# First weight sums of the down projections: added by GpSimd's DMAs from DRAM to DRAM instead of by VectorE, and three more seven-product pairs

## The chip, the cores and the metric

The kernel runs on one core of one Trainium2 chip. The metric is the device time of one execution in microseconds; of the kernel before there are three runs: 2095.61, 2094.24 and 2094.99 us, median 2094.99.

## What is computed

A two-layer encoder trunk on one sequence of 256 tokens, width 2048, all in float32. Per layer: an RMS norm, one input projection, a token mixer (layer 0 differential attention, layer 1 windowed grouped-query attention with a sink) beside four heads that attend to 256 memory tokens, an output projection, and an MLP with squared ReLU. Cut to what the change touches:

```python
for i in range(DEPTH):                      # 2 layers
    h = rms_norm(x, norm_attn[i])
    proj = h @ w_in_a[0]                    # layer 0: 2048 x 5120; layer 1: w_in_b, 2048 x 3072
    ...                                     # heads, memory heads (w_mem_kv)
    x = x + heads @ w_out[i]                # 2048 x 2048
    h = rms_norm(x, norm_mlp[i])
    x = x + jnp.square(jax.nn.relu(h @ w_up[i])) @ w_down[i]   # 2048 x 8192, then 8192 x 2048
```

## The kernel before, in words

**Products in three passes.** Every float32 operand is split into a rounded part and a rest (`split`, L411 to L413: ScalarE copies `hi`, VectorE subtracts to get `lo`), and each product is three TensorE matmuls (`three`, L503: hi by hi, hi by lo, lo by hi). Weights come from DRAM in pieces of 512 KB (128 partitions x 1024 float32), by DMAs that SyncE issues (`fetch`, L389) into four buffers `raw`; four `hi` and four `lo` buffers follow. The order of the pieces is one long plan (L254 to L259): per layer the input projection (`a`, 80 pieces, or `b`, 48), the memory projection (16 pieces), `out`, `up` (128 pieces), `down` (128 pieces). A piece of an input projection feeds 12 matmuls of 512 columns (`chunk_tok`, L453 to L469).

**Down projection.** Each half of the output columns (h = 0, 1) goes through 32 pairs of pieces (j = 0 to 31). A pair is a 2 x 2 block product for two column chunks and two token tiles: normally eight block products, 24 matmuls (`one_of_eight`, L508). For the pairs in `FAST` (L48; `LATE`, L49, for the second half of layer 0) it is done with seven products, 21 matmuls (`seven`, L521), in the manner of Strassen and Winograd. These need two sums of weights, a and b, and differences of the hidden values. There are 15 + 13 + 15 + 15 = 58 such pairs.

**Weight sums.** For a seven-product pair `load_pair` (L316) has SyncE load the first piece whole into a slot of the tile `big`. `sum_pair` (L336) makes a (first piece, its two halves, each plus the upper half of the second piece: `first_sum`, L281, one VectorE addition over 1024 columns), then b by two additions over 512 columns, and splits both. For 19 of the 58 pairs (`MADE`, `MADE_LATE`: 5 + 4 + 5 + 5) a is not made there: `make_sum` (L284) loads the three halves a second time during the up projection, adds on VectorE (L302, the same L282), and GpSimd's DMAs store the sum to DRAM (`madesum`, L307, two of 256 KB). `load_pair` then loads that sum (512 KB) and only the lower half of the second piece (256 KB, tile `t2k`), instead of the whole second piece. A pair whose sum is in DRAM so takes 1.25 MB of loads, any other 1 MB.

**Hidden differences.** `keep` (L962) makes the differences of the hidden values for every pair j that is a seven-product pair in either half, during the up projection, and a GpSimd DMA stores them (`kept`, L967, 512 KB); in the down projection a GpSimd DMA loads them (L1038). Six buffers `h2` carry both, and the split hidden values.

**Order.** PE, VectorE, ScalarE, GpSimd and SyncE each have one queue. The program text interleaves side work with the pieces through a small planner: `tick` is called once per piece in the input projections, and a `Task` does its next stage when its wait, counted in ticks, is over; `Light` stages are done beside the others. That sets the place in the text. The build then lays each engine's instructions out by when their inputs and buffers are there; where a load or an operation must not come earlier than its place, the text says so with `tc.issue_after` (L292, L377, L745, L755, L824, L1079, L852), which queues it behind a named instruction of the same engine.

**Bias.** Around the place of the change in layer 0, GpSimd also makes position distances (`bias_distance`, L751) and issues 32 DMAs of 128 KB (`bias_hot`, L796) for the relative-position bias. TensorE multiplies what they bring (`bias_rows`, L806).

Of the kernel before, what the change touches and what calls it, by code (L numbers as in the profile page):

```python
# [14 lines left out]
F32 = mybir.dt.float32  # L15
# [4 lines left out]
ALU = mybir.AluOpType  # L20
# [24 lines left out]
SINGLE = 4  # L45
AHEAD = 2
WARM = 10
FAST = (1, 3, 5, 7, 9, 11, 13, 15, 17, 19, 21, 23, 25, 27, 29)  # L48
LATE = (3, 5, 7, 9, 11, 13, 15, 17, 19, 21, 23, 25, 27)  # L49
AWAY = range(6, 12)  # L50
LATE_BLK = (9, 13, 17, 21, 25)
LOOK = 2
KEEP_AFTER = (2, 6)
MADE_GAP = 1
MADE = (3, 9, 15, 21, 27)
MADE_LATE = (7, 13, 19, 25)
LAM_INIT = 0.8 - 0.6 * math.exp(-0.3 * 0)

G_ATTN, G_MEM, G_MLP = 0, 2 * KT, 4 * KT
# [9 lines left out]
def trunk(ctx: ExitStack, tc: tile.TileContext, xin, xtok, memin, memtok, posrel, gcol, rows,  # L69
# [43 lines left out]
    def t2k(shape, dt=F32):  # L113
        return tp.tile(shape, dt, tag="t2k", name=nm("t2k"), bufs=6)
# [127 lines left out]
            return LATE if (name, h) == ("down0", 1) else FAST  # L242
        return ()

    def made_pairs(name, h):

        if name.startswith("down"):
            return MADE_LATE if (name, h) == ("down0", 1) else MADE
        return ()

    def plan_pairs(name, n):
        plan.extend((name, h, j) for h in range(2) for j in range(2 * n))

# [27 lines left out]
    def first_sum(a, first, upper):  # L281
        nc.vector.tensor_tensor(a, first.rearrange("p (a n) -> p a n", a=2), upper.unsqueeze(1).broadcast_to([P, 2, 512]), op=ALU.add)  # L282

    def make_sum(name, h, j):  # L284

        box = {}

        def load(i):
            if i == 0:
                box["raw"] = quad("h2", (P, 1024), F32), t2k([P, 512])  # L290
            first, upper = box["raw"]
            with tc.issue_after(behind[0].ins):  # L292
                if i < 2:
                    nc.sync.dma_start(first[:, i * 512:(i + 1) * 512], weights[name][h, 2 * j][:, i * 512:(i + 1) * 512])
                else:
                    nc.sync.dma_start(upper, weights[name][h, 2 * j + 1][:, 512:1024])

        def add():
            first, upper = box["raw"]
            box["a"] = quad("h2", (P, 2, 512), F32)  # L300
            box["kept"] = dp.tile([P, 2, 512], F32, name=nm("madesum"))
            first_sum(box["a"], first, upper)  # L302
            made_in[name, h, j] = box["kept"]
            save(0)

        def save(i):
            nc.gpsimd.dma_start(box["kept"][:, i, :], box["a"][:, i, :])  # L307

        return Task([lambda: load(0), lambda: load(1), lambda: load(2), add, lambda: save(1)], gap=MADE_GAP)

    made_in = {}
    hidden_in, hids = {}, {}
# [639 lines left out]
    def mlp(layer, X2, last):  # L952
        hT = []
        kept = {}
        wide = big([P, 6, 4, S])
        slots.clear()
        slots.extend(wide[:, c - 6] for c in AWAY)
        hidden_in.clear()
        def hidden(j):
            return hT[j // 2].rearrange("p k s -> p (k s)")[:, (j % 2) * 512:(j % 2) * 512 + 512]  # L960

        def keep(j):  # L962

            t2 = quad("h2", (P, 2, 512))
            differences(t2, hidden(j))
            kept[j] = dp.tile([P, 2, 512], F32R, name=nm("kept"))
            nc.gpsimd.dma_start(kept[j], t2)  # L967

        to_make = [(f"down{layer}", h, j) for h in range(2) for j in made_pairs(f"down{layer}", h)]
        for c in range(16):  # L970
            for i in range(len(to_make) * c // 13, len(to_make) * (c + 1) // 13):
                if i < len(to_make):
                    make_sum(*to_make[i])
            ps = chunk_out(f"up{layer}", c, 8, lambda k: X2[k], "mm" if c % 2 == 0 else "aux", 2 if c == 0 else 1)
            if c == 0:
                mlp_stats()
            ht = wide[:, c - 6] if 6 <= c < 12 else blk([P, 4, S], F32)
            for o in range(4):
                t = t1k()
                nc.scalar.copy(t, ps[o][:, 256:512])  # L980
                nc.vector.tensor_tensor(t, ps[o][:, 0:256], t, op=ALU.add)
                nc.vector.scalar_tensor_tensor(ht[:, o, :], t, 0.0, t, op0=ALU.max, op1=ALU.mult)
            hT.append(ht)
            if c in AWAY:
                for i in range(2):
                    hidden_in[2 * c + i] = dp.tile([P, 512], F32, name=nm("hid"))
                    nc.gpsimd.dma_start(hidden_in[2 * c + i], hidden(2 * c + i))
            for j in (2 * c, 2 * c + 1):
                if any(j in fast_pairs(f"down{layer}", h) for h in range(2)):
                    Task([Light(lambda j=j: keep(j), 0)], wait=KEEP_AFTER[j % 2])  # L990
        N2 = Halves()

        def h2_of(j):
            t2 = quad("h2", (P, 2, 512))
            split(t2[:, 0, :], t2[:, 1, :], hids.pop(j) if j in hidden_in else hidden(j))
            return lambda kk, t, part: t2[:, part, kk * S + t * P:kk * S + (t + 1) * P]

        flush()

        for half_ in range(2):  # L1000
            tag = "mm" if half_ == 0 else "aux"
            ps = [[bank(tag) for _ in range(2)] for _ in range(2)]
            chunks = (2 * half_, 2 * half_ + 1)
            fast = fast_pairs(f"down{layer}", half_)

            def add_to(n, t, src, i=0):
                at = chunks[n] * 512 + i
                d = xt[:, t, at:at + src.shape[1]]
                nc.vector.scalar_tensor_tensor(d, src, r2[:, t:t + 1], d, op0=ALU.mult, op1=ALU.add)
                return at, d  # L1010

            def finish(n, t, src, i=0):
                at, d = add_to(n, t, src, i)
                if last:
                    nc.sync.dma_start(out[:, t * D + at:t * D + at + src.shape[1]], d)

            def by_columns(n, t):

                for i in (0, 256):
                    part_ = bank("mm")[:, 0:256]  # L1020
                    for j, two, at in held:
                        for kk in range(2):
                            three(part_, j == held[0][0] and kk == 0, j == held[-1][0] and kk == 1,
                                  lambda part: at(kk, t, part), two[(kk + n) % 2], slice(n * 512 + i, n * 512 + i + 256))
                    finish(n, t, part_, i)

            held = []
            for j in range(32):
                if j == fast[0]:
                    side = [bank("aux" if half_ == 0 else "mm") for _ in range(4)]  # L1030
                two = [piece(f"down{layer}", half_, 2 * j + i) for i in range(2)]
                at = h2_of(j)
                if last and half_ == 1 and j >= 30:
                    held.append((j, two, at))
                    continue
                if j in fast:
                    t2 = quad("h2", (P, 2, 512))
                    nc.gpsimd.dma_start(t2, kept[j])  # L1038
                    seven(ps, side, j == fast[0], j == fast[-1], two, sums.pop((f"down{layer}", half_, j)), at, t2)
                else:  # L1040
                    for kk in range(2):
                        for t in range(2):
                            for n in range(2):
                                own_last = 2 * fast[-1] - 1 if last and half_ == 1 and n == t == 1 else 4 * KT - 1
                                one_of_eight(ps, n, t, 2 * j + kk, own_last, two, at)
                if j == fast[-1]:
                    shared(side, add_to)
                    if last and half_ == 1:
                        add_to(1, 1, ps[1][1])
                tick()  # L1050
                tick()
            for n in range(2):
                for t in range(2):
                    if held and n == t == 1:
                        by_columns(n, t)
                        continue
                    for j, two, at in held:
                        for kk in range(2):
                            one_of_eight(ps, n, t, 2 * j + kk, 4 * KT - 1, two, at)
                    finish(n, t, ps[n][t])  # L1060
                if not last:
                    chunk_sq(chunks[n])
                    to_features(chunks[n], N2, G_ATTN + KT, tag)
        return N2

# [27 lines left out]
    rows_done = [Task([lambda i=i: bias_hot(i), lambda i=i: bias_rows(i, bias)], [prep], wait=BW, gap=BGAP) for i in range(8)]  # L1093
    Task([lambda: bias_save(bias)], rows_done)
    H2 = Halves(lambda pair: "h2" if pair < 6 else "x2")
    loads = Task([lambda c=c: load_residual(c) for c in range(4)], wait=RES_AT, gap=RES_GAP, front=True)
    for g in range(3):
        if g == 2:
# [29 lines left out]
    st1 = cp.tile([P, 4], F32, name="st1")  # L1128
    H2 = Halves(lambda pair: "h2" if pair < 6 else "x2")
    bias = bias_load()  # L1130
    ps = chunk_tok("b", 3, X2, steps=2)
    row_stats(st1)
    kT, kd = norm_T(ps, st1, 4, gc[:, G_BK:G_BK + 1])
# [82 lines left out]
```

## Time and profile before

| what | value |
|---|---|
| runs | 2095.61, 2094.24, 2094.99 us |
| span of the profiled execution (its own time, from first to last instruction) | 2092.7 us |
| median of the runs less that span | 2.3 us |
| DVE (VectorE) busy | 1640.3 us, 78% |
| ACT (ScalarE) busy | 1173.6 us, 56% |
| POOL (GpSimd) busy | 103.0 us, 5% |
| DMA | 506.29 MB, mean 242 GB/s |
| input projection and memory projection, layer 0 | about 5 to 320 us |
| up projection, layer 0 | 415 to 772 us |
| down projection, layer 0 | 772 to about 1119 us |

Start and length of the profiled execution are read from the trace; the runs are timed without it, and the 2.3 us between them lie around the span. "Busy" of PE is matmuls that overlap, with modelled ends, so two things are read beside it: the idle time of PE, and the distance between the starts of two matmuls in a row. "us to landing" of a DMA runs from its issue to its last byte. "DMA share" is the mean busy share of the core's 16 DMA engines (it can come out a little over 1 in a short stretch). A queue q0 is GpSimd's, q1 is SyncE's.

### The profile page before, as it was taken

The page shows a single profiled execution, that of the slowest core. Times are in us where ns is not written, and L with a number is a line of the kernel's source. Part 1 is how long each engine was busy: PE and PEld are TensorE (multiplying, and loading weights), DVE is VectorE, ACT ScalarE, POOL GpSimd, SP SyncE. Part 2 cuts the span into 40 slices and gives each one's busy share as a digit, 9 for nine tenths or more (in the row PEclk, how much of TensorE's full clock was granted, in tenths as well). Part 3 has the DMA queues.
Part 4 walks back from the last instruction along what each step waited for, and adds up shares of the span by engine and source line. Part 5 has one row for each costly group of instructions (what it writes and reads, how often), then busy time and mean ns, then how long its engine had stood idle before and what let it go on. Part 6 is the DMA issues. An engine that isn't in the chain of part 4 may idle for free.

```text
span 2092.7 us, 30004 instructions
## 1 busy us (share of the span) xinstructions
PE 2088.2 (100%) x10920; PEld 1773.8 (85%) x10920; DVE 1640.3 (78%) x2467; ACT 1173.6 (56%) x1776; POOL 103.0 (5%) x193
## 2 busy tenths in 40 slices
PE   9999999999999999999999999999999999999999
PEld 8888888888888888888888888888888888888887
DVE  7667778866666679999986677886676667999998
ACT  7467665544444456666655566564444445666664
POOL 1200000000011000000000000000010100000000
PEclk9999999999999999999999999999999999999999
DMA  9666654577789778878866555457788877888884
GB/s 320 241 204 200 194 161 161 186 241 251 251 298 310 238 264 274 293 246 268 303 243 197 178 171 178 149 194 250 252 272 299 307 231 277 273 288 289 284 294 145
DMA packets 150995, 506.29 MB, mean 242 GB/s; under 512 B 17856, under 2 KB 18880, under 8 KB 150592
## 3 DMA queue, kind: packets, MB, share of 16 engines
q1 hardware_dynamic: 131536, 437.78, 63.1%
q0 software_dynamic: 19168, 66.60, 9.5%
q8 instruction: 85, 1.39, 0.3%
q14 instruction: 62, 0.51, 0.1%
q10 hardware_dynamic: 144, 0.01, 0.0%
HBM read 466.96 MB, written 37.36 MB: 241 GB/s over the span
## 4 chain that ended last, share of the span: by engine, by line
PE 100%; DVE 0%; issue 0%
PE mm L478 11%; PE aux L478 11%; PE mm L465 7%; PE mm L466 7%; PE mm L467 7%; PE mm L505 7%; PE mm L506 7%; PE mm L504 7%; PE aux L506 7%; PE aux L505 7%; PE aux L504 7%; PE mm L482 6%; PE aux L482 6%; PE aux L600 1%; PE aux L577 1%; PE aux L619 1%
## 5 line engine op out<-in xcount | busy, mean ns | idle before, releaser
L413 DVE TENSOR_TENSOR lo<-raw,hi 128x1024 fp32r<-128x1024 f32 (+1 forms) x616 | 738.6, 1210 | 365.3 <-ACT hi L412 361.0
L412 ACT CAST hi<-raw 128x1024 fp32r<-128x1024 f32 (+1 forms) x616 | 632.0, 1040 | 592.4 <-PE mm L478 158.2
L465 PE MATMUL mm<-hi,x 128*128 128x512 f32 x640 | 256.5, 403 | 0.0
L466 PE MATMUL mm<-lo,x 128*128 128x512 f32 x640 | 251.3, 393 | 0.0
L467 PE MATMUL mm<-hi,x 128*128 128x512 f32 x640 | 250.4, 392 | 0.2 <-DVE x L409 0.2
L478 PE MATMUL mm<-x,hi 128*128 128x512 f32 x1024 | 246.9, 391 | 0.0
L478 PE MATMUL aux<-x,hi 128*128 128x512 f32 x1024 | 246.9, 391 | 0.0
L478 PEld LDWEIGHTS mm<-x,hi 128*128 128x128 f32 x1024 | 188.3, 188 | 36.3
L478 PEld LDWEIGHTS aux<-x,hi 128*128 128x128 f32 x1024 | 188.3, 188 | 36.3
L412 ACT CAST x<-big 128x1024 fp32r<-128x1024 f32 x106 | 110.6, 1053 | 141.6 <-DVE big L345 114.9
L504 PE MATMUL mm<-hi,h 128*128 128x512 f32 (+1 forms) x454 | 176.1, 388 | 0.0
L505 PE MATMUL mm<-lo,h 128*128 128x512 f32 (+1 forms) x454 | 176.0, 388 | 0.0
L506 PE MATMUL mm<-hi,h 128*128 128x512 f32 (+1 forms) x454 | 176.0, 388 | 0.0
L504 PE MATMUL aux<-hi,h 128*128 128x512 f32 x440 | 171.5, 390 | 0.0
L506 PE MATMUL aux<-hi,h 128*128 128x512 f32 x440 | 171.2, 390 | 0.0
L505 PE MATMUL aux<-lo,h 128*128 128x512 f32 x440 | 171.2, 389 | 0.0
L467 PEld LDWEIGHTS mm<-hi,x 128*128 128x128 f32 x640 | 120.3, 188 | 26.3 <-DVE x L409 0.5
L465 PEld LDWEIGHTS mm<-hi,x 128*128 128x128 f32 x640 | 120.6, 189 | 23.8
L466 PEld LDWEIGHTS mm<-lo,x 128*128 128x128 f32 x640 | 120.8, 189 | 23.0 <-DVE lo L413 1.0
L482 PEld LDWEIGHTS aux<-x,lo 128*128 128x128 f32 x1024 | 131.3, 191 | 5.0
L482 PEld LDWEIGHTS mm<-x,lo 128*128 128x128 f32 x1024 | 131.1, 191 | 4.8
L482 PE MATMUL mm<-x,lo 128*128 128x256 f32 x1024 | 133.0, 283 | 0.0
(270 smaller groups left out, 3101.8 us busy)
## 6 DMA issues: line engine op xcount, KB each, us to landing
raw<-in_w_up SPq DMA_DIRECT2D x256, 512.0 KB, 4.6
raw<-in_w_down SPq DMA_DIRECT2D x140, 512.0 KB, 4.7
big<-in_w_down SPq DMA_DIRECT2D x97, 512.0 KB, 5.0
raw<-in_w_a SPq DMA_DIRECT2D x72, 512.0 KB, 3.7
h<-kept POOLq DMA_DIRECT2D x58, 512.0 KB, 6.0
raw<-in_w_out SPq DMA_DIRECT2D x52, 512.0 KB, 4.0
raw<-in_w_b SPq DMA_DIRECT2D x48, 512.0 KB, 3.7
raw<-in_w_mem SPq DMA_DIRECT2D x32, 512.0 KB, 3.6
```

The lines of the kernel that those rows point to most:

```text
L412: nc.scalar.copy(hi, src)
L413: return nc.vector.tensor_tensor(lo, src, as32(hi), op=ALU.subtract)
L465: nc.tensor.matmul(ps[t], lhsT=xh, rhs=hi[:, ws], start=(k == 0), stop=False)
L466: nc.tensor.matmul(ps[t], lhsT=xh, rhs=lo[:, ws], start=False, stop=False)
L467: nc.tensor.matmul(ps[t], lhsT=xl, rhs=hi[:, ws], start=False, stop=(k == KT - 1))
L478: nc.tensor.matmul(ps[o], lhsT=hi[:, cols(k % 2, o)], rhs=x2.rearrange("p a s -> p (a s)"), start=(k == 0), stop=(k == 2 * nj - 1))
L482: nc.tensor.matmul(ps[o][:, 256:512], lhsT=lo[:, cols(k % 2, o)], rhs=x2[:, 0, :], start=False, stop=False)
L504: nc.tensor.matmul(acc_, lhsT=x(0), rhs=w2[0][:, ws], start=first_, stop=False)
L505: nc.tensor.matmul(acc_, lhsT=x(0), rhs=w2[1][:, ws], start=False, stop=False)
L506: nc.tensor.matmul(acc_, lhsT=x(1), rhs=w2[0][:, ws], start=False, stop=last_)
L577: nc.tensor.transpose(out=pt[:, h * P:(h + 1) * P], in_=qn[t][:, h * P:(h + 1) * P], identity=ident)
L600: nc.tensor.transpose(out=pt[:, kt * S + qt * P:kt * S + (qt + 1) * P], in_=p_of(qt)[:, kt * P:(kt + 1) * P], identity=ident)
```

## The change

The first sums of all seven-product pairs of the down projections are made in DRAM. `make_sums` replaces `make_sum`: for each pair a GpSimd DMA copies the first piece (512 KB) from the weights to a new DRAM tile, and a second GpSimd DMA adds the upper half of the second piece to both halves of that tile (an accumulating DMA, the source read twice). The text puts copy i one step after copy i-1 and together with addition i-1, a step every three ticks, from tick 20 of layer 0 for `down0` (29 pairs) and from two ticks into layer 1 for `down1` (32 pairs). No `tc.issue_after` stands around them. `FAST` has 16 pairs instead of 15, with two places where neighbours follow each other (9, 10 and 18, 19); `LATE` is as before: 16 + 13 + 16 + 16 = 61 pairs. `make_sum` and its 19 tasks in the up projections go.

```diff
-FAST = (1, 3, 5, 7, 9, 11, 13, 15, 17, 19, 21, 23, 25, 27, 29)
+FAST = (1, 3, 5, 7, 9, 10, 12, 14, 16, 18, 19, 21, 23, 25, 27, 29)
...
-MADE_GAP = 1
-MADE = (3, 9, 15, 21, 27)
-MADE_LATE = (7, 13, 19, 25)
+SUM_GAP = 3
+SUM_AT = (20, 2)
...
-    def make_sum(name, h, j):
...
+    def make_sums(name, at):
+
+        def copy(h, j):
+            made_in[name, h, j] = dp.tile([P, 2, 512], F32, name=nm("madesum"))
+            nc.gpsimd.dma_start(made_in[name, h, j].rearrange("p a n -> p (a n)"), weights[name][h, 2 * j])
+
+        def add(h, j):
+            upper = weights[name][h, 2 * j + 1][:, 512:1024]
+            nc.gpsimd.dma_start(made_in[name, h, j], upper.unsqueeze(1).broadcast_to([P, 2, 512]), accum_op=ALU.add)
+
+        def step(i):
+            if i:
+                add(*wanted[i - 1])
+            if i < len(wanted):
+                copy(*wanted[i])
+
+        wanted = [(h, j) for h in range(2) for j in fast_pairs(name, h)]
+        return Task([Light(lambda i=i: step(i), SUM_GAP) for i in range(len(wanted) + 1)], wait=at, gap=SUM_GAP)
...
-        to_make = [(f"down{layer}", h, j) for h in range(2) for j in made_pairs(f"down{layer}", h)]
         for c in range(16):
-            for i in range(len(to_make) * c // 13, len(to_make) * (c + 1) // 13):
-                if i < len(to_make):
-                    make_sum(*to_make[i])
...
         N2 = Halves()
+        flush([summed[layer]])
...
+    summed = [make_sums("down0", SUM_AT[0])]
     loads = Task([lambda c=c: load_residual(c) for c in range(4)], wait=RES_AT, gap=RES_GAP, front=True)
...
+    summed.append(make_sums("down1", SUM_AT[1]))
     ps = chunk_tok("b", 3, X2, steps=2)
```

More of the change, by code (lines that the diff above doesn't have):

```diff
@@ L243, in fast_pairs @@
         return ()
[L245 to L249, printed above, removed]
     def plan_pairs(name, n):
@@ L282, in first_sum @@
         nc.vector.tensor_tensor(a, first.rearrange("p (a n) -> p a n", a=2), upper.unsqueeze(1).broadcast_to([P, 2, 512]), op=ALU.add)
-    def make_sum(name, h, j):
[L286 to L309, printed above, removed]
+    def make_sums(name, at):
[12 more added lines that the diff above has]
+        return Task([Light(lambda i=i: step(i), SUM_GAP) for i in range(len(wanted) + 1)], wait=at, gap=SUM_GAP)
     made_in = {}
```

## The prediction, made before the result was known

> **What bounds the kernel now.** I read the page, then busy time by stretch, then TensorE's timeline in a down projection.
>
> ```profile
> span 2092.7 us, 30004 instructions
> ...
> PE 2088.2 (100%) x10920; PEld 1773.8 (85%) x10920; DVE 1640.3 (78%) x2467; ACT 1173.6 (56%) x1776; POOL 103.0 (5%) x193
> ```
>
> ```profile
> 415.00:772.00 357.00, 357.00 (x2061) 315.84 (x2060) 236.79 (x337) 167.38 (x225) 25.31 (x47) 1.00 0.80 265
> 772.00:1119.00 347.00, 347.00 (x1549) 287.74 (x1548) 319.48 (x377) 220.53 (x289) 16.77 (x28) 1.00 0.80 267
> ```
>
> ```profile
> 772.53 0.39 PE L504 MATMUL mm<-hi,h 128*128 128x512 f32 x1
> ...
> 777.97 0.39 PE L504 MATMUL aux<-hi,h 128*128 128x512 f32 x1
> ...
> 782.73 0.39 PE L504 MATMUL mm<-hi,h 128*128 128x512 f32 x1
> ```
>
> The columns of a stretch are its length, then busy time of PE, weight loads, VectorE, ScalarE and GpSimd, the granted clock, the DMA share and GB/s. PE is without idle time through the whole up projection (357.00 of 357.00) and down projection (347.00 of 347.00). The timeline shows that it isn't slowed unseen either: pair 0, with eight products, starts at 772.53 and pair 1, with seven, at 777.97. That is 5.44 us for 24 matmuls, and 4.76 us for pair 1's 21: both 0.2267 us a matmul, one behind the other. So this kernel ends when TensorE has done its matmuls. Time goes only by fewer matmuls, and comes only by a stall.
>
> **The change part by part.**
>
> *Three more pairs.* Each saves 5.44 - 4.76 = 0.68 us; three save 2.04 us. This is the only part that takes anything off TensorE.
>
> *Sums taken off VectorE.*
>
> ```profile
> L282 DVE TENSOR_TENSOR big<-big 128x1024 f32<-128x1024 f32 x39 | 47.5, 1219 | 0.0
> ...
> L282 DVE TENSOR_TENSOR h<-h,t2k 128x1024 f32<-128x1024 f32 x19 | 23.2, 1219 | 0.0
> ```
>
> 47.5 + 23.2 = 70.7 us of VectorE work go. No PE idle time stood behind it, so it is worth nothing by itself. It pays for the three new pairs: with a ready-made sum a seven-product pair no longer has this 1.22 us.
>
> *Loads in the down projection.* 42 pairs change from 1 MB to 1.25 MB, and three new pairs also load differences of 0.52 MB: 42 x 0.262 + 3 x 0.524 = 12.6 MB over some 680 us, 18 GB/s on top of 267, at a DMA share of 0.80. That makes about 0.86, and I cost it at nothing; loads stand two pairs ahead. Six more differences are made in the up projections (five in layer 0 for the even pairs), beside VectorE that is busy 237 of 357 us there: nothing. If the cover were gone at the two places where seven-product pairs are neighbours, it would be a microsecond or so each.
>
> *The 122 new DMAs.* All of the risk is here: when do they run, and beside what? First, when. The copies read weights and write fresh DRAM tiles: they wait for nothing. How does the build treat an instruction that is ready sooner than its place in the text? VectorE, ScalarE and GpSimd show it:
>
> ```profile
> 18.68 0.15 DVE L838 TENSOR_SCALAR gs<-gc 128x1 f32<-128x1 f32 x1
> ...
> 19.24 0.61 DVE L780 CAST tab<-posrel 128x48 bf16<-128x48 f32 x1
> ...
> 22.69 0.42 DVE L756 CAST t2k<-t2k 128x512 f32<-128x512 int32 x1
> ```
>
> ```profile
> 757.09 0.62 ACT L412 CAST h<-t2k 128x512 fp32r<-128x512 f32 x1
> 757.62 2.18 ACT L412 CAST h<-blk 128x512 fp32r<-128x512 f32 x4
> ```
>
> ```profile
> 18.50 1.30 POOL L751 TENSOR_TENSOR t2k<-posrel,rw 128x256 int32<-128x256 int32 x2 [17.19 <-DMA posrel<-in_posrel]
> ...
> 44.78 4.32 POOL L796 DMA_DIRECT2D blk<-bkt  x8 [24.69 <-DMA bkt<-t1k]
> 49.39 1.05 POOL L796 DMA_DIRECT2D blk<-bkt  x2 [0.29 <-DMA blk<-bkt]
> ```
>
> L780 stands at tick 17 in the text, six stages behind L756 (which is held back on purpose), and runs at 19.24, before it, as soon as its input has landed. The four hidden splits of pairs 0 to 3 run at 757.62, all at once behind the last `keep`, though pair 3 is used only from 777.97 + 4.76 + 5.44 = 788 us. So ticks don't hold an instruction; inputs and buffers do, and for the copies there are none. GpSimd is idle until 18.50. I therefore expect the copies at the head of GpSimd's queue, from about 1.5 us, for both layers, with the additions among them. What limits them is the count in flight: L796 issues eight DMAs, and the ninth waits for a landing. So GpSimd would keep up to eight of them open until all 61 x 2 x 0.524 = 64 MB are through.
>
> Second, beside what.
>
> ```profile
> 0.00:10.00 10.00, 8.94 (x36) 7.63 (x37) 4.23 (x9) 5.88 (x10) 0.69 (x6) 1.00 0.75 222
> 10.00:20.00 10.00, 10.00 (x46) 8.24 (x45) 9.99 (x26) 8.55 (x19) 1.50 (x3) 1.00 1.06 387
> 20.00:30.00 10.00, 10.00 (x46) 8.29 (x45) 9.19 (x21) 6.16 (x12) 0.09 (x1) 1.00 1.04 398
> ```
>
> Between 10 and 30 us the DMA engines are full (share 1.04 to 1.06) with SyncE's own loads at 387 and 398 GB/s, and TensorE lives on them. What GpSimd takes there is taken from TensorE. How much is it? From 48 to 66 us GpSimd has its 128 KB bias DMAs queued beside the weights (the queues of that stretch, then SyncE's weight load over the whole run):
>
> ```profile
> q1 hardware_dynamic: 1010, 3.69, 52.0%
> q0 software_dynamic: 1123, 3.05, 47.7%
> ...
> raw<-in_w_a SPq DMA_DIRECT2D x7, 512.0 KB, 6.8
> blk<-bkt POOLq DMA_DIRECT2D x24, 128.0 KB, 5.6
> ```
>
> ```profile
> raw<-in_w_a SPq DMA_DIRECT2D x72, 512.0 KB, 3.7
> ```
>
> The engines are shared about half and half; SyncE gets 3.69 MB in 18 us, 205 GB/s, GpSimd 169, and a weight load takes 6.8 us instead of 3.7. At 169 GB/s the 64 MB last 376 us. Now the sum, at the 23rd piece (four L465 matmuls each; the second row is all engines):
>
> ```profile
> 0.00:73.50 73.50, 35.45 (x92) 17.45 (x92) 1.00 0.93 330
> ```
>
> ```profile
> 73.50:290.00 216.50, 216.50 (x1339) 177.49 (x1339) 160.30 (x411) 137.74 (x302) 0.00 (x0) 1.00 0.59 190
> ```
>
> ```profile
> L413 DVE TENSOR_TENSOR lo<-raw,hi 128x1024 fp32r<-128x1024 f32 (+1 forms) x616 | 738.6, 1210 | 365.3 <-ACT hi L412 361.0 <-DMA big<-in_w_down 1.2
> L412 ACT CAST hi<-raw 128x1024 fp32r<-128x1024 f32 (+1 forms) x616 | 632.0, 1040 | 592.4 <-PE mm L478 158.2 <-PE aux L478 155.2 <-PE mm L467 122.4
> ```
>
> By 73.50 us 92 / 4 = 23 pieces are multiplied. SyncE must have brought 23 x 0.524 = 12.1 MB of weights, 2.1 MB of x by features, 2.1 MB of x by tokens and 0.3 MB of rows: 16.6 MB. At 205 GB/s that is 81 us, and behind the last load come 1.04 + 1.21 us of splitting and 12 x 0.2267 = 2.7 us of matmuls: 86.0 instead of 73.5, +12.5 us. After that the stage asks for 190 GB/s, under 205, so it grows no further.
>
> *Bias behind the sums.* L751 and the 32 bias DMAs stand in the same GpSimd queue, and a bias DMA would queue behind up to eight sums: 8 x 0.524 MB at 169 GB/s, 25 us.
>
> ```profile
> L806 PE MATMUL aux<-tab,blk x384: 182/183/198, 61.3 to 102.7; 128*128 128x48 bf16 x192
> ```
>
> The first one is issued at 44.78 now and its matmuls start at 61.3: some 11 us to spare behind a landing of 5.6 us, and TensorE is itself later by 12 us. 25 - 11 - 12 is about nothing, but the position load that the chain starts with (L751) also comes later, by 5 to 10 us. I take +5, between 0 and +10.
>
> Sum, made on the span: 2092.7 - 2.0 + 12.5 + 5.0 = 2108.2. The 2.3 us between span and median stay: 2110.5 us.
>
> *Bounds.* No row shows a copy from DRAM to DRAM or an accumulating DMA. Below: they could take less than the bias DMAs do, down to nothing; a gain beyond 2.04 us is excluded, as there is no PE idle time to win. Above: the mean of SyncE's own queue over the run,
>
> ```profile
> q1 hardware_dynamic: 131536, 437.78, 63.1%
> ```
>
> is 437.78 MB in 0.631 x 2092.7 us, 332 GB/s, half of it 166: 16.6 MB take 100 us, +31.5 at the 23rd piece, and to 290 us another 216.5 x (190/166 - 1) = 31, with +10 for the bias 2166 us. I take 205, the nearest row: GpSimd's DMAs beside this very stage. My own mechanism's range is 2098 to 2150.
>
> [...]
>
> **The rivals.**
>
> *Not slower: the sums run where the text puts them.* If something holds them to tick 20 (about 60 us) and beyond, and in layer 1 to 1119 us, one copy and one addition are open at a time. The start-up is over by then, and the stages ask for less than the 205 GB/s that a half leaves them:
>
> ```profile
> 1119.00:1300.00 181.00, 180.84 (x898) 152.21 (x897) 129.33 (x257) 101.31 (x184) 0.00 (x0) 1.00 0.57 178
> ```
>
> No stall, and the three pairs stay: 2095.0 - 2.0 = 2093.0 us. It is decided by the first copy's issue: 50 us or later. For it speaks only that the rows above show instructions moved by some 30 us, not by hundreds.
>
> [...]
>
> *Slow additions.* An addition also reads its target. If its bytes take twice the engine time, the weights get 125 GB/s beside it, 159 on average: +36 at the 23rd piece, +42 up to 290 us, with the bias 2176 us. Nothing in the trace speaks against it.
>
> **How the numbers follow.** My case 0.52, small packets 0.10, in place 0.28, slow additions 0.10. A measurement of this kernel can tell about 0.2%, 4.2 us. Only the case in place falls within that, and no case gives more than 2 us of gain: faster 0.01, same 0.28, slower 0.71. The range must hold the case in place and my own up to 2150; the slow additions are left out: 2092 to 2150. The slower cases alone: 2098 to 2150.
>
> **What would show it.** Right: `madesum` DMAs issued on GpSimd from the first microseconds, weight loads of `w_a` landing in 7 us or more at the median, PE idle time before 100 us, L796 later than 44.78 us; up and down projections as long as now, less 2 us. Wrong: first `madesum` issue beyond 50 us and PE without idle time (2093); or a PE that waits far past 300 us (slow additions); or idle time in the down projections near pairs 9, 10, 18, 19.

## The result and the profile after

The changed kernel takes 2163.43 us (median of 5 runs, 2159.99 to 2164.34) against 2094.99: slower, ratio 1.0325 (95% interval 1.0313 to 1.0338). The forecast was 2110.5 and its range ended at 2150. The profiled execution was the shortest of the five (2159.99 us); its span is 2158.2 us, 65.5 more than before.

In the changed kernel L281 is the copy, L285 the addition, L374 the load of a weight, L397 and L398 its split on ScalarE and VectorE, L450 to L452 the products of the input projections. First the page, then busy time by stretch (columns as in the prediction), of the changed kernel and, the last two rows, of the kernel before:

```profile
span 2158.2 us, 30093 instructions
...
PE 2115.5 (98%) x10911; PEld 1783.2 (83%) x10911; DVE 1590.0 (74%) x2445; ACT 1183.8 (55%) x1788; POOL 184.1 (9%) x286
...
PEclk9899999989999999999999999999999999999999
```

```profile
0.00:100.00 100.00, 78.99 (x320) 57.58 (x320) 50.34 (x93) 43.44 (x76) 30.00 (x52) 0.90 1.01 317
100.00:290.00 190.00, 180.45 (x1202) 147.79 (x1203) 124.64 (x306) 106.51 (x230) 48.92 (x67) 0.98 1.05 326
290.00:460.00 170.00, 162.89 (x799) 133.14 (x797) 125.39 (x254) 95.65 (x195) 35.69 (x45) 0.97 1.04 318
460.00:1119.00 659.00, 657.82 (x3378) 563.94 (x3379) 497.04 (x663) 365.29 (x477) 32.10 (x60) 0.99 0.78 260
```

```profile
0.00:100.00 100.00, 98.94 (x730) 81.96 (x731) 74.42 (x128) 59.29 (x99) 19.82 (x41) 1.00 0.82 284
100.00:290.00 190.00, 190.00 (x1050) 155.17 (x1049) 141.55 (x384) 124.73 (x284) 0.00 (x0) 1.00 0.60 195
```

TensorE, idle for 1.1 us of the first 290 before, now stands idle for 21.0 us of the first 100, 9.6 of the next 190 and 7.1 of the next 170; from 460 to 1119 us it is idle for 1.2 us. The DMA engines are full in just these stretches (1.01, 1.05 and 1.04, against 0.60 before in the second). And the granted clock, 1.00 before, is 0.90, 0.98 and 0.97. So there are two losses: idle time, 21.0 - 1.1 + 9.6 + 7.1 = 37 us, and slow matmuls, at most 10 + 3.8 + 5.1 = 19 us (where TensorE is idle at half clock, the clock costs nothing). Together that is up to 56 of 65.5; the clock falls once more at 461 us, and gaps shorter than a matmul's drawn length of 0.39 us don't show as idle time.

How the stream runs, by GpSimd's timeline (start, duration, line), the tile's summary (count, durations, first and last start) and the groups of instructions:

```profile
1.29 0.66 POOL L281 DMA_DIRECT2D madesum<-in_w_down  x1 [0.35 <-issue]
...
6.88 1.11 POOL L285 DMA_DIRECT2D madesum<-in_w_down  x1 [4.53 <-DMA madesum<-in_w_down]
7.51 1.98 POOL L281 DMA_DIRECT2D madesum<-in_w_down  x3
18.55 1.08 POOL L285 DMA_DIRECT2D madesum<-in_w_down  x1 [9.06 <-DMA madesum<-in_w_down]
```

```profile
L281 POOL DMA_DIRECT2D madesum<-in_w_down x61: 655/983/1925, 1.3 to 422.5; - x61
L285 POOL DMA_DIRECT2D madesum<-in_w_down x61: 1021/1051/1637, 6.9 to 442.3; - x61
```

```profile
L285 POOL DMA_DIRECT2D madesum<-in_w_down x61 | 64.2, 1071 | 294.6 <-DMA madesum<-in_w_down 290.5 <-issue 3.7
```

The first copy goes at 1.29 us, and the sums of both layers follow at once: the last addition starts at 442.3 us, long before layer 1 begins. But they go in groups of three. An addition must wait for its copy to land (290.5 us of waiting in all), and what stands behind the addition on GpSimd waits too: the next three copies start at 7.51 us, behind the 4.53 us that the first addition waited.

Now the queues, up to 104 us (where the 23rd piece's load has landed), then in the middle of the stream; and the weight load over the whole run:

```profile
q1 hardware_dynamic: 8188, 18.55, 51.0%
q0 software_dynamic: 4049, 14.56, 49.5%
```

```profile
q0 software_dynamic: 14061, 49.28, 61.0%
q1 hardware_dynamic: 14125, 54.07, 44.0%
```

```profile
raw<-in_w_a SPq DMA_DIRECT2D x72, 512.0 KB, 8.7
```

```profile
0.00:108.30 108.30, 39.16 (x92) 19.48 (x92) 0.91 1.01 322
```

In the start-up the engines are shared in halves, as forecast, but SyncE's half brings 18.55 MB in 104 us, 178 GB/s. The 23rd piece (92 matmuls of L452) is done by 108.3 us, not 73.5: +35. Between 120 and 440 us the second fence gives GpSimd 61.0% and SyncE 44.0%, 54.07 MB in 320 us, 169 GB/s, where the stage asks for 190. A weight load takes 8.7 us instead of 3.7.

One such wait in the timeline, and how its name misleads:

```profile
177.32 1.04 ACT L397 CAST hi<-raw 128x1024 fp32r<-128x1024 f32 x1 [4.17 <-DMA raw<-in_w_a]
178.40 1.23 DVE L398 TENSOR_TENSOR lo<-raw,hi 128x1024 fp32r<-128x1024 f32 x1 [4.09 <-ACT hi L397]
179.54 0.88 DVE L625 SCALAR_TENSOR_TENSOR t2k<-t2k,sm 128x256 f32<-128x256 f32 x2
...
180.08 0.33 PE L585 MATMUL aux<-ident,t2k 128*128 128x128 f32 x1 [3.98 <-DVE t2k L625]
```

TensorE waits 3.98 us for a step of the attention (L625). That step isn't slow: it stands on VectorE behind the split of a weight (L398), which waited 4.09 us for ScalarE, which waited 4.17 us for the load. Follow such a wait back along the waiting engine until a DMA ends it.

### The profile page after: what moved, and what is told of

The parts are those of the page before. It is cut to its first block, busy times and chain, and to the rows that moved or that the text cites. A ratio compares the mean times of both kernels' runs of the same rounds, so it can differ in the third digit from the quotient of the medians.

```text
span 2158.2 us, 30093 instructions
## 1 busy us (share of the span) xinstructions
PE 2115.5 (98%) x10911; PEld 1783.2 (83%) x10911; DVE 1590.0 (74%) x2445; ACT 1183.8 (55%) x1788; POOL 184.1 (9%) x286
## 3 DMA queue, kind: packets, MB, share of 16 engines
q0 software_dynamic: 35968, 125.32, 19.9%
## 4 chain that ended last, share of the span: by engine, by line
PE 88%; DMA 8%; DVE 2%; ACT 1%; issue 1%; SPq 0%; ACTq 0%; DVEq 0%
PE mm L463 11%; PE aux L463 11%; PE aux L491 6%; PE aux L490 6%; PE mm L491 6%; PE aux L489 6%; PE mm L489 6%; PE mm L490 6%; PE mm L467 6%; PE aux L467 6%; DMA raw<-in_w_a 5%; PE mm L450 5%; PE mm L451 5%; PE mm L452 5%; DMA raw<-in_w_out 1%; DVE lo L398 1%
## 5 line engine op out<-in xcount | busy, mean ns | idle before, releaser
L398 DVE TENSOR_TENSOR lo<-raw,hi 128x1024 fp32r<-128x1024 f32 (+1 forms) x610 | 732.9, 1212 | 474.3 <-ACT hi L397 472.0
L397 ACT CAST hi<-raw 128x1024 fp32r<-128x1024 f32 (+1 forms) x610 | 625.8, 1039 | 690.6 <-PE aux L463 177.5
L450 PE MATMUL mm<-hi,x 128*128 128x512 f32 x640 | 262.4, 412 | 15.8 <-ACT hi L397 15.3
L451 PE MATMUL mm<-lo,x 128*128 128x512 f32 x640 | 257.1, 402 | 4.6 <-DVE lo L398 4.4
L452 PE MATMUL mm<-hi,x 128*128 128x512 f32 x640 | 254.8, 398 | 0.0
L489 PE MATMUL mm<-hi,h 128*128 128x512 f32 (+1 forms) x443 | 172.0, 389 | 0.8 <-ACT hi L397 0.8
L491 PE MATMUL mm<-hi,h 128*128 128x512 f32 (+1 forms) x443 | 171.6, 389 | 0.1
L450 PEld LDWEIGHTS mm<-hi,x 128*128 128x128 f32 x640 | 123.0, 193 | 44.6 <-ACT hi L397 19.8
L452 PEld LDWEIGHTS mm<-hi,x 128*128 128x128 f32 x640 | 123.2, 193 | 26.5
L397 ACT CAST x<-big 128x1024 fp32r<-128x1024 f32 x112 | 114.1, 1050 | 45.9 <-DVE big L330 45.9
L398 DVE TENSOR_TENSOR x<-big,x 128x1024 fp32r<-128x1024 f32 x112 | 136.5, 1220 | 0.0
```

The costliest lines, as they stand in the source:

```text
L397: nc.scalar.copy(hi, src)
L398: return nc.vector.tensor_tensor(lo, src, as32(hi), op=ALU.subtract)
L450: nc.tensor.matmul(ps[t], lhsT=xh, rhs=hi[:, ws], start=(k == 0), stop=False)
L451: nc.tensor.matmul(ps[t], lhsT=xh, rhs=lo[:, ws], start=False, stop=False)
L452: nc.tensor.matmul(ps[t], lhsT=xl, rhs=hi[:, ws], start=False, stop=(k == KT - 1))
L489: nc.tensor.matmul(acc_, lhsT=x(0), rhs=w2[0][:, ws], start=first_, stop=False)
```

## The experiments

**Is it the bytes, or the new order of the instructions?**

```
-  nc.gpsimd.dma_start(made_in[...], weights[name][h, 2 * j])
+  nc.gpsimd.dma_start(made_in[...][0:8], weights[name][h, 2 * j][0:8])
   (the addition likewise; the load of a sum reads the weights instead)
```

> Same instructions in the same order on every engine; copies and additions move only the first 8 of the 128 rows of each sum (4 MB in place of 64), and the down projections load unsummed weights where the sums would be (as many bytes; this part of the computation is left out). Theory SHARE (the bytes of the copies and additions take DMA engine time from SyncE's weights, TensorE idles and then runs at half clock for a while): the whole loss goes, 2095.0 - 2.0 = 2093, between 2091 and 2098. Rival ORDER (the instructions were put in another order on TensorE, VectorE and GpSimd, the bias rows later and elsewhere, and that costs): the time stays above 2130.

2096.56 us, ratio 1.0007 (0.9997 to 1.0016).

```profile
0.00:100.00 100.00, 98.53 (x726) 81.01 (x727) 74.11 (x128) 59.49 (x99) 56.49 (x94) 1.00 0.88 300
```

The forecast of 2091 to 2098 holds. With 122 DMAs in the same order, but a sixteenth of the bytes, TensorE is busy and its clock is full. The order costs nothing to speak of; 67 of the 68 us go with the bytes (and with the large packets, which this kernel doesn't have either).

**Copies, writes, additions, packets.** Three kernels with the instructions in the same order:

```
copies_whole    addition for rows 0:8 only
plain_writes -  nc.gpsimd.dma_start(..., accum_op=ALU.add)
             +  nc.gpsimd.dma_start(...)
small_packets - dp.tile([P, 2, 512])
              + dp.tile([P, 1040])[:, 0:1024]
```

> Same order; copies are whole, the additions move 8 of 128 rows (the rest of the sums is left out). Packets of the changed kernel: 976 copy packets of 1213 ns are 74 us on each of 16 engines, 15616 addition packets of 176 ns are 172 us. Theory SHARE with the additions as the larger part: GpSimd holds about 40% of the engines while the copies last (some 185 us), SyncE keeps 0.6 x 345 = 207 GB/s, the 16.6 MB of the start-up take 80 + 5 us, +12, with some clock loss 2108 (2100 to 2118). Rival BIG PACKETS (a 32 KB packet holds an engine seven times as long as a 4 KB packet of weights, so the copies do the harm): nearly all of the loss stays, above 2140. Rival BYTES (only the bytes count): about half of the loss, 2128.

> Same order and same bytes issued; the second DMA writes the upper half over the copy and doesn't add (the addition is left out). A plain 2 KB packet takes 84 ns in the changed kernel's trace, an adding one 176: 82 us of engine time in place of 172. Theory SHARE: about 40 of the 70 us stay, 2133 (2115 to 2145), and the stream ends near 310 us, not 460. Rival BYTES or BIG PACKETS: adding costs nothing by itself, 2155 to 2163.

> Same order, same computation; each sum lies in rows of 1040 numbers, so a copy goes in 128 packets of 4 KB and not in 16 of 32 KB. Theory SHARE with the additions as the larger part: the copies take as much engine time as before in smaller turns, a little is won, 2150 (2140 to 2162). Rival BIG PACKETS: most of the loss goes, below 2130. Rival BYTES: 2163, no change.

Copies alone: 2116.57 (ratio 1.0107, 1.0079 to 1.0135). Writing instead of adding: 2149.87 (1.0272, 1.0238 to 1.0305). Copies in 4 KB packets: 2145.30 (1.0240, 1.0225 to 1.0255). The copies of the first kernel and the second DMAs of the other two (behind the durations the first and the last start):

```profile
L281 POOL DMA_DIRECT2D madesum<-in_w_down x61: 666/817/1230, 1.3 to 248.6; - x61
```

```profile
L285 POOL DMA_DIRECT2D madesum<-in_w_down x61: 648/666/1055, 6.7 to 358.7; - x61
```

```profile
L285 POOL DMA_DIRECT2D madesum<-in_w_down x61: 1122/1151/2027, 6.7 to 450.0; - x61
```

The copies cost 20 us beyond the kernel with a sixteenth of the bytes, the second DMA 33 more as a plain write, and adding instead of writing 14 more. The four runs of the copies lie between 2110.5 and 2125.5, those of the plain writes between 2144.8 and 2162.6, so these parts are known to some 7 us only. SHARE's forecasts held within their ranges for the copies, at the upper end (22 us above before, not 13), and for the small packets, and failed for the plain writes: adding by itself is the smallest of the three parts, though by the packet records of the changed kernel's trace an adding packet of 2 KB does take 176 ns of an engine at the median, where one of SyncE's plain 2 KB loads takes 84. The plain write isn't quite the same DMA either: its queue has 28160 packets against 35968, 61 x 128 fewer, so it goes in 4 KB pieces; what of the 14 us is adding and what the smaller pieces isn't separated.

The packets' size counts for itself: the same bytes and the same sums, with the stream no shorter (450 us), and 18 us less lost. A copy's 32 KB packet (1213 ns) holds an engine 7.6 times as long as a weight's 4 KB packet (159 ns). None of the 18 us comes from the start-up, though. Here are the products of the first 23 pieces, and SyncE's queue between 120 and 440 us, with 4 KB packets:

```profile
0.00:108.30 108.30, 37.81 (x92) 18.88 (x92) 0.89 1.00 322
```

```profile
q1 hardware_dynamic: 15057, 57.49, 46.0%
```

The 23rd piece is done at 108.3 us as in the changed kernel, and behind it SyncE gets 57.49 MB instead of 54.07, 180 GB/s instead of 169. So the bytes do most of the harm and the big packets some of it, later; neither BYTES nor BIG PACKETS holds with its number. The pitch of the sums in DRAM changed together with the packets, and was not tried by itself; an adding packet takes the same 176 ns at both pitches.

**Start-up or rate?** VectorE copies a flag out of the newest split weight, GpSimd copies the flag, and the sum's DMAs stand behind that:

```
+ nc.vector.tensor_copy(f, newest[0][:, 0:1])
+ held[0] = nc.gpsimd.tensor_copy(g, f)
+ with tc.issue_after(held[0].ins):
      add(...); copy(...)
paced: for each step (layer 1: 24 sums)    first_held: for the first, from tick 33
start_free: from the 11th on (layer 1: 24 sums)
```

> Each step of the sums waits, by a flag that VectorE copies out of the newest split weight, for the piece at which the text puts it: first copy at about 60 us, one copy and one addition about every 10 us; the last 8 of layer 1's 32 sums are made on VectorE, since the stage has no room for them. A sum took 442/61 = 7.2 us of the queue when it ran free, so SyncE has the engines alone for about a quarter of the time and gets some 220 GB/s on average against the 190 that the stage asks. Theory SHARE: no stall of weight, 2093 (2091 to 2099), no loss of clock. Rival STEADY (an addition beside the weights delays single pieces by itself, at whatever pace): idle time near the copies, 2105 or more.

> The first copy of each layer waits by such a flag (layer 0 at about 105 us, layer 1 at about 1125 us); behind it all run free, as in the changed kernel. Nothing runs beside the start-up. Theory SHARE: a stage that asks for 190 GB/s and gets 170 loses on: the changed kernel lost 10 us from 100 to 290 and 16 from 290 to 460 beyond the kernel before, 0.074 us per us; 29 x 7.2 = 210 us of it in layer 0 and 32 x 7.2 = 230 in layer 1 make 16 + 17, 2126 (2110 to 2140). Rival START (only the start-up loses, where the DMA engines were full before): 2093 to 2100.

> The opposite: the first 10 sums run free from the first microsecond (about 72 us), all others are paced as in the paced kernel (the last 8 of layer 1 on VectorE). Theory SHARE: the start-up loses what it lost in the changed kernel, 34 us by 100 us, and nothing later: 2127 (2117 to 2135). Rival RECOVERED (a delay of the start-up is mostly made good later): under 2110.

2104.93 (ratio 1.0054, 1.0042 to 1.0067), 2131.38 (1.0182, 1.0166 to 1.0198) and 2135.06 (1.0194, 1.0180 to 1.0206). Paced, two stretches; first held, its second stretch; start free, two:

```profile
0.00:100.00 100.00, 98.71 (x690) 81.54 (x691) 73.89 (x130) 58.69 (x98) 25.63 (x52) 1.00 0.91 309
100.00:290.00 190.00, 190.00 (x1091) 154.77 (x1091) 144.15 (x405) 124.79 (x285) 34.01 (x55) 1.00 0.97 296
```

```profile
100.00:290.00 190.00, 180.42 (x972) 145.93 (x971) 127.84 (x349) 114.55 (x261) 43.01 (x57) 0.97 1.04 323
```

```profile
0.00:100.00 100.00, 80.59 (x376) 60.13 (x377) 53.56 (x98) 45.51 (x79) 31.85 (x56) 0.90 1.00 313
100.00:290.00 190.00, 190.00 (x1239) 155.96 (x1238) 137.49 (x350) 116.84 (x252) 18.50 (x33) 1.00 0.79 249
```

One sum every 10 us fits beside the weights of layer 0: TensorE is busy for 190.00 of 190.00 us at a DMA share of 0.97, and starts the last matmul of layer 0's projections at 320.08 us, where the kernel before does so at 319.64. Three in a row without a pause don't fit: 9.6 us idle at 1.04, with no start-up involved. The first ten alone cost 2135.06 - 2104.93 = 30 us beyond the paced kernel, a hair above their range (2135): the 23rd piece is 31.6 us late, the last of layer 0's projections 31.7. Held, the stream costs 37, within its range: at the end of layer 0's projections 16 us are lost, at the end of layer 1's (1340.97 us instead of 1306.29) 35. START falls, as the rate alone costs time with no sum in the start-up, and RECOVERED too. That 30 and 37 make about what the change cost is partly chance: about half of the 37 arises in layer 1, where the changed kernel makes no sums, and behind its 23rd piece that kernel loses 30 us in layer 0 alone.

The paced kernel is 12 us above its forecast, though, at the 2105 of STEADY; but STEADY's idle time near the copies is missing in layer 0. Nearly all of its loss lies at one place: at 1104 us it is 0.4 us behind the kernel before, at the end of layer 1's projections 9.3 (1315.57 against 1306.29). Between the two stands its one long wait, TensorE's row first, then ScalarE's between 1230 and 1285 us:

```profile
PE mm L465 <- ACT x L408: 4.9, 1, 4.9
```

```profile
ACT x L408 <- DMA h<-in_memin: 11.0, 2, 7.2
```

A load of memory tokens stands on SyncE's queue there, behind a row of weight loads, beside open sums; a stretch at half clock follows near 1270 us.

**What does idle time do to the clock?** In the kernel before, TensorE is made to wait for GpSimd seven times:

```
+ first_ = matmul(one, lhsT=ones, rhs=ones); nc.scalar.copy(s, one)
+ for _ in range(n): nc.gpsimd.tensor_tensor(s, s, s, op=add)
+ matmul(one, lhsT=s, rhs=ones)        # n = 2, 4, 6, 8, 10, 14, 18
```

> The kernel before, with seven stalls put into TensorE between 150 and 330 us: a matmul waits for a chain of 2, 4, 6, 8, 10, 14 and 18 small GpSimd operations that starts from the matmul ahead of it (about 1 to 9 us each). No other work is added or moved. Theory CLOCK: an idle time of 2 to 4 us makes the granted clock fall to 0.5 for 3.41 or 6.83 us behind it, with every one of the longer stalls, none with the shortest; each costs 1.7 or 3.4 us beyond the stall itself. Rival LOAD (the clock fell in the changed kernel because of its DMA traffic, not of the idle time): the clock stays at 1.00.

2145.1 us, one run. Around the second stall (TensorE idle until 194.46 us, 1.8 us in one piece):

```profile
192.00:195.80 3.80, 1.75 (x9) 1.34 (x9) 3.31 (x12) 2.03 (x8) 2.18 (x4) 1.00 0.29 50
195.80:199.20 3.40, 3.40 (x10) 2.17 (x8) 0.00 (x0) 0.00 (x0) 0.00 (x0) 0.50 0.32 125
199.20:203.00 3.80, 3.80 (x19) 3.17 (x19) 1.23 (x1) 1.05 (x1) 0.00 (x0) 1.00 0.13 17
```

In the second row TensorE is busy for all of 3.40 us and does 10 matmuls; in the third, at full clock, 19 in 3.80. The shortest stall, about 1 us, left the clock alone; the six others brought 3.41, 6.83, 3.41, 6.83, 10.24 and 6.83 us at half clock. That is 37.6 us. Busy time of TensorE in the six stretches, and in the nine that the changed kernel has, from the sums over these windows:

```profile
sum 37.40, PE 28.12 PEld 22.27 DVE 8.72 ACT 4.58 POOL 9.14; mean PE 4.69 PEld 3.71 DVE 1.45 ACT 0.76 POOL 1.52
```

```profile
sum 44.20, PE 40.57 PEld 30.61 DVE 32.15 ACT 24.35 POOL 7.25; mean PE 4.51 PEld 3.40 DVE 3.57 ACT 2.71 POOL 0.81
```

Half of the busy time is lost: 14 us here, beside 31 us of idle time, together 45 of the 50 that the kernel lost (the rest, with the added matmuls in it, I can't assign), and 20 us in the changed kernel. DMA share is about 0.3 or less there, so LOAD falls, and CLOCK holds, with one longer stretch (10.24) than forecast.

It is not the single gap that counts, though. Around the changed kernel's last stretch, and a longer wait that brought none, in the kernel with the first copy held (2.46 us; granted clock 1.00 from 137.8 to 144.6 us):

```profile
457.80:461.20 3.40, 1.87 (x7) 0.81 (x5) 2.09 (x2) 2.37 (x3) 0.00 (x0) 1.00 0.13 47
461.20:468.00 6.80, 6.06 (x15) 4.62 (x15) 6.80 (x9) 5.46 (x7) 0.00 (x0) 0.50 0.38 90
```

```profile
142.21 0.33 PE L599 MATMUL aux<-ident,t2k 128*128 128x128 f32 x1 [2.46 <-DVE t2k L639]
```

No gap before 461.2 us is longer than 0.8 us, but the 3.4 us ahead of it are busy for only 1.87. Ahead of all fifteen stretches TensorE was busy for 1.9 of the last 3.41 us or less; the gap of 2.46 us falls into two stretches of that length, which are busy for 1.95 and 2.39 us. The border isn't sharp: the 3.41 us ahead of 177.9 us in the changed kernel, busy for 1.6, brought no slow stretch.

In the kernel with the stalls, and in the changed one, all stretches begin at whole multiples of 3.41 us from one another (in the changed kernel at 20.9, 51.6, 65.3, 72.1, 181.3, 218.9, 304.2, 444.1 and 461.2 us). One gap of 1.8 us was enough, and so were two of 0.8.

**Can the idle time be filled?**

```
+ if clock[0] < 28:
+     for i in range(5): nc.tensor.matmul(idle, lhsT=hi[:, 0:P], rhs=hi[:, 0:512])
```

> The changed kernel with five more matmuls (5 x 0.227 = 1.13 us, result unused) behind each of the first 28 pieces, 32 us of work for a TensorE that loses 38 us there; they fill its idle time, so that its clock need not fall. Theory ABSORBED (in the start-up the weights set the pace, and a slower clock only shortens the next wait): the 23rd piece still ends its way at 108 us and the time stays at 2163, within 4. Theory ADDED (the half clock costs its 10 us of the start-up on top of the waits): the 23rd piece some 10 us sooner, 2153.

2177.21 us (ratio to before 1.0396, 1.0382 to 1.0410), 14 more than the changed kernel.

```profile
0.00:127.90 127.90, 38.48 (x92) 18.91 (x92) 0.92 1.00 305
```

Neither theory: the 23rd piece is done 19.6 us later, of 23 x 1.13 = 26 us put in, and the clock fell all the same (0.92; in the first 100 us 0.90, as in the changed kernel). So in the start-up TensorE's own time still counts, by some three quarters, though it waits for weights again and again. I read it so: a load is issued only when an earlier piece's buffer is free, so a late TensorE makes the next load late; that wasn't tried by itself, and the added matmuls also hold a piece's `hi` and a bank longer. How much of the half clock's cost in the start-up comes through stays open.

**Is there anything to win?** Layer 1's DMA-made sums end ahead of its memory projections (12 of 32, others on VectorE); and the kernel before with 61 pairs and no DMA-made sums:

```
paced2    MADE_MOST = {"down0": 29, "down1": 12}
before61  FAST = (1, 3, 5, 7, 9, 10, 12, 14, 16, 18, 19, 21, 23, 25, 27, 29)
          MADE = (3, 10, 16, 19, 25)
```

> As the paced kernel, but only the first 12 of layer 1's sums are made by DMA (the last copy near 1243 us, ahead of layer 1's memory projections); the other 20 are made on VectorE. In the paced kernel the one stall left, 5 us and a stretch at half clock near 1270 us, stood behind a load of memory tokens on SyncE's queue while sums were open. Theory SHARE: without sums there the stall goes, 2093 (2091 to 2097). Rival OTHER (that stall comes from the other order or from 61 pairs, not from the sums): 2102 or more.

> The kernel before with the changed kernel's 61 pairs; the first sums are made as before, by VectorE (19 of them during the up projections, 42 beside the products). If VectorE has the room, the three pairs bring the same 2.04 us without any sum made by DMA: 2093 (2091.5 to 2094.3). Rival VECTOR (at the neighbouring pairs 9 and 10, 18 and 19 VectorE is late, as it has 1.22 us more to do there): 2096 or more.

2103.01 (ratio 1.0040, 1.0028 to 1.0052; runs from 2098.04 to 2109.39) and 2094.82 (1.0001, 0.9992 to 1.0009). The long wait of layer 1 shrank to 1.1 us, as SHARE had it, yet the median fell by only 2 us, no run came within SHARE's 2091 to 2097, and OTHER's "2102 or more" fits the time. The profiled run, 2100, has small waits that before doesn't have, most of them in the down projections. ScalarE waits there for ready-made sums to come back (460 to 1119 us):

```profile
ACT blk L412 <- DMA big<-madesum: 17.4, 5, 4.8
```

But the changed kernel has the same row with 15.0 us, and no more idle time there than 1.2 us, so this row doesn't explain the loss. What does, and what makes its runs differ by 11 us, stays open. The second kernel missed its forecast (2091.5 to 2094.3) by 0.5 us and stays below its rival's 2096. It shows why the prize was so small. Pairs 9 and 10 of the down projection, both with seven products:

```profile
831.98 0.40 PE L504 MATMUL aux<-x,h 128*128 128x512 f32 x1
832.21 0.39 PE L505 MATMUL aux<-x,h 128*128 128x512 f32 x1
832.61 0.96 PE L506 MATMUL mm<-hi,h 128*128 128x512 f32 x3
```

0.40 us from one matmul to the next instead of 0.23, and 0.11 more at the next: some 0.3 us. Such gaps stand at five of the six places where two such pairs are neighbours, and give back 1.5 of the 2.04 us. The changed kernel, whose sums were ready long before, has them at all six, so they don't come from the first sums, and no placing of these could have won 2 us. What they wait for stays open.

## Why the prediction was wrong

- *What bounds the kernel, and VectorE's 70.7 us worth nothing*: right. VectorE's busy time fell from 1640 to 1590 us, and nothing came of it.
- *Copies at the head of GpSimd's queue, for both layers*: right, 1.29 us against the 1.5 forecast. *Eight open, 376 us in all*: wrong. The additions wait for their copies and go in groups of three, and the last one starts at 442 us.
- *Half and half in the start-up, +12.5*: the mechanism is right, 51.0% against 49.5%; the term measured +35. By 104 us SyncE had brought 18.55 MB where I had added up 16.6 (parts of the pieces behind the 23rd come along), which at 205 GB/s would be +22; and its half brought 178 GB/s and not 205, which makes the rest. The row that I took was one of nothing but 4 KB packets on both queues; in the start-up 8 of SyncE's 18.55 MB, x and the half loads of weights, go in packets of 2 KB. That this explains the lower rate was not tried.
- *"After that the stage asks for 190 GB/s, under 205, so it grows no further"*: this is the step that failed. The stream left SyncE 44.0% and 169 GB/s, and the loss grew from 35 us at piece 23 to 53 at the last piece of layer 0's projections (372.7 us against 319.6) and to 65.2 by the end of the output projection (479.5 us against 414.3), after which it stayed. A margin of 15 GB/s on a figure from 18 us of other DMAs was no margin. The upper bound, half of SyncE's mean rate, 166 GB/s, was the better row, and I cut the range below it. That its sum, 2166, is only 3 us off is luck: it holds 10 us for the bias, which cost nothing, and nothing for the clock.
- *Bias +5*: no such term. The bias DMAs start at 79.7 us instead of 44.8, but TensorE is as late as they are, and waits for their rows 0.5 us in all.
- *Extra loads in the down projections at nothing*: right within a microsecond or two in the changed kernel. *Three pairs, -2.04*: wrong, about -0.2 by the six gaps, and in the time of the kernel with 61 pairs nothing (2094.82 against 2094.69); I had named the neighbours and given them no cost.
- *Not in the sum at all*: the clock. Once idle time was forecast, the matmuls behind it had to be priced too; some 20 us, within the two losses above.
- *The rivals.* In place: nothing held the sums; paced by a flag they take 2103 to 2105 us and not 2093, as the pairs bring nothing and in layer 1 a load comes late beside them. Small packets: no run shows that additions in 2 KB packets leave the weights more than half. They do go in packets of 2 KB, but one takes 176 ns, more than a weight's 4 KB (159), the copies go in packets of 32 KB, and SyncE was left 169 GB/s. Slow additions: its premise is right (176 ns against 84) and its sum, 2176, is the nearest of the rivals, but adding made only 14 of the 68 us; plain copies and writes already made 53.

## What to carry to other kernels

Here DMAs without a dependency started at once, far from their place in the text: ask what the first microseconds and the busiest stage have to spare, and pace it by a real dependency if it must not run there. When two queues compete, take the share from what the new transfers are (packet size, reads and writes), and let the range reach to the stall if the demand lies near the share: here the share came out at 169 GB/s where 205 was forecast, and the demand was 190. Price a stall with the slow clock that follows it (here 14 us beside 31 us of stalls), and a gain of 2 us with the places where its cover is thinnest.

## What was not expected of the hardware

TensorE's clock halved in fifteen places, for 3.41, 6.83 or 10.24 us, each time behind 3.41 us in which TensorE had been idle for 1.5 us or more, once in one gap of 1.8 us and once in two of 0.8; in the kernel with the stalls that added 14 us to 31 us of idle time. An accumulating DMA from DRAM to DRAM took an engine 176 ns for 2 KB, a plain load 84. A copy of 512 KB from DRAM to DRAM between contiguous tiles went in packets of 32 KB; with 4 KB packets, had by nothing but a pitch of 1040 numbers, the kernel lost 18 us less.
